# A hybrid decoder layer on one core: x instead of E at the start, more gate strips ahead of the GLU, E behind the recurrence, the last products on VectorE

## Chip, core and metric

One core of a Trainium2 chip. The metric is the device time of one execution in microseconds (us), from inputs in HBM to the output in HBM. PE is TensorE, PEld its weight loads, DVE is VectorE, ACT is ScalarE, POOL is GpSimd, SP the engine whose queue issues the DMAs.

## The reference

One layer on 1024 tokens of width 1024, batch 1, in float32 (the names are the reference's; shapes are left out):

```python
h = rms_norm(x, g_mix)
z = h @ w_in + b_in                      # 3584 columns: u_a 512, u_b 1024, gate_a 1024, gate_b 1024
y_a = s5_mixer(u_a)                      # diagonal complex SSM, then gelu and a GLU
y_b = rglru_mixer(u_b)                   # causal conv of 4, gates r and i per head, a linear recurrence
x = x + (gate_a * (y_a @ w_a_out) + gate_b * (y_b @ w_b_out)) @ w_o
h2 = rms_norm(x, g_ffn)
x = x + (silu(h2 @ w_ffn_gate) * (h2 @ w_ffn_up)) @ w_ffn_down
gate_p = sigmoid(rms_norm(x, g_ple_gate) @ w_ple_gate + b_ple_gate)
e = rms_norm(p @ w_ple, g_ple)
x = x + gate_p * e
return rms_norm(x, g_final)
```

## The kernel before

Everything is held transposed: 128 channels on the partitions, 1024 tokens along the free axis. A tile of 128 x 1024 float32 is a slot of SBUF (43 slots), and a PSUM tile of that size is one of four PSUM slots. A *strip* is 128 output channels of a product: its weights are 8 blocks of 128 x 128, loaded in two halves of 256 KB into three raw buffers.

Each factor is split in two: ScalarE makes a high part (`whi`, `xgh`, line 190 or 237), VectorE the rest (`wlo`, `xgl`, line 191 or 238). `mm3` (line 215) then does three products per block, each in two matmuls of 512 tokens, so a strip of w_in is 8 x 3 x 2 = 48 matmuls and a product of E, which has two blocks of p, is 12.

`plan` writes the work down as a list of units, in the order in which PE is to take them. `emit` (line 323) issues a unit: its weights' loads and splits a few halves ahead (`load_to`, `prep_to`), its matmuls, after the first half the evacuation of the unit before (`flush`), and after each half one `tick`, which takes every running chain (a Python generator, such as the norm's or the S5 branch's) one step further. So a chain's place among the strips is counted in ticks of 24 matmuls. Within the first `HEAD_UNITS` units, ScalarE and VectorE keep the order in which this is written; for the rest, and for PE, POOL and SP throughout, a planner fixes each engine's order before the run, by the order of issue, by when it expects the data and by `high_priority`. Each engine then works strictly in its order, and an instruction that waits holds back all behind it.

The order before is:

- **E**, p @ w_ple: eight units of 12 matmuls (lines 496 to 511). `head` (line 471) issues all loads: p, w_ple, the small tables, x. Meanwhile a chain (`x_one`, line 459) splits the eight tiles of x and sums their squares, and the S5 parameters start on POOL (`s5_params`, line 1161, instructions on 16 columns). The results go to HBM (`ed`).
- **u_a**, four strips of w_in. Their evacuation needs the norm of x (`rstd_chain`, line 370): sums on PE, the power `rs` on POOL (line 388), `dg` on VectorE, a product with ones that spreads it (line 395), and ScalarE's copy `rb` (line 400). The S5 parameters that follow are issued behind `rs`.
- **Ten gate strips** (`GATES_FIRST`), while the S5 branch runs as chains: setup of two halves (`s5_setup`, line 1319), sine tables, input products (line 1451), rotation and scans on VectorE, output products (line 1488), four steps apart (`S5_LAG`). Up to here that is 8 x 12 + 14 x 48 = 768 matmuls of `mm3`.
- The **GLU** (4 strips of 24), the first u_b strip (UB 0), and w_a_out.
- The **recurrence**: UB 1 to 7, behind UB m the gate pair `ri` of m - 2, and a gate strip behind m = 2, 3, 5, 6 (`UB_GATES`). A UB strip is evacuated by VectorE, ScalarE and VectorE again (convolution, `xc`) and split (`xch`). Each pair of channels' tiles then goes through `lru` (line 609): exponential, tanh, square root on ScalarE, products and two scans on VectorE. Behind `ri` 6 there is a gate strip, `ri` 7, and one more gate strip; then w_b_out, which needs the splits of all y_b.
- w_o, the FFN, w_down, and the gate of E at the end, whose last five strips are cut at token 768 (`TAIL_CUT`): the first part's final norm (`final_head`, line 995) runs beside the second parts' matmuls. `final_mul` (line 990) is the product of a finished tile with the final norm and its store; before, four of the first six are on POOL and two on VectorE (`FIN_FIRST`), and two more wait for `final_tail` (`FIN_LAST`).

Of the kernel before, what the change touches and what calls it, by code (L numbers as in the profile page):

```python
# [15 lines left out]
ALU = mybir.AluOpType  # L16
# [17 lines left out]
GATES_FIRST = 10  # L34
UB_GATES = (2, 3, 5, 6)
RI_LAG = 2
S5_LAG = 4
S5_STAGGER = 3
X_POOL = ()
HEAD_UNITS = 10  # L40
# [4 lines left out]
FIN_FIRST = ((0, 0), (1, 1), (2, 0), (3, 1), (4, 1), (5, 1))  # L45
FIN_LAST = (6, 7)
# [41 lines left out]
class WUnit:  # L88
# [3 lines left out]
    def __init__(self, strips, ops, out, pre=None):  # L92
        self.strips, self.ops, self.out, self.pre = strips, ops, out, pre
        self.first = None
        self.raw = self.sums = None


class Build:
# [223 lines left out]

    def emit(self, u, ahead):
        if isinstance(u, WUnit):
# [113 lines left out]
    def plan(self):  # L438
# [11 lines left out]
        pt = {}  # L450

        def p_tile(k):
            return pt[k]

        xg = {}
        xacc = []
        st = {}

        def x_one(k):
            t = st.pop(("x", k))  # L460
            xg[k] = self.split(t, "xg", scale=self.v("g_mix", k))
            self.accum(xacc, t, nc.gpsimd if k in X_POOL else nc.vector)

        def x_chain():
            for k in range(8):
                x_one(k)
                yield

        wple = {}

        def head():
            t = [self.slot(name="p") for _ in range(2)]
            nc.sync.dma_start(t[0], h["pT"][0])
            self.s5p = self.small([P, 48], name="s5p")
            self.dd = self.small([32, 16, 16], name="dd")
            for i in range(2):
                wple[i] = self.slot(name="wple")
                nc.sync.dma_start(wple[i][:, :512], h["w_ple"][2 * i])
                if i == 0:
                    nc.sync.dma_start(t[1], h["pT"][1])  # L480
                    nc.sync.dma_start(self.vec, h["vec"])
                    nc.sync.dma_start(self.s5p, h["s5p"])
                    nc.sync.dma_start(self.dd, h["s5d"])
                    nc.sync.dma_start(self.ident, h["ident"])
                    nc.sync.dma_start(self.iota, h["iota"])
                nc.sync.dma_start(wple[i][:, 512:], h["w_ple"][2 * i + 1])
                for k in range(4 * i, 4 * i + 4):
                    st["x", k] = self.slot(name="x")
                    nc.sync.dma_start(st["x", k], h["xT"][k])
            for k in range(2):  # L490
                pt[k] = self.split(t[k], "p")
                self.prep_to(1)
            self.xc = self.start(x_chain())
            self.start(self.s5_all())

        def ev_e(n):
            def ev(ps):
                t = self.slot(name="e")
                if n % 2:
                    nc.scalar.activation(out=t, in_=ps, func=AF.Copy)  # L500
                else:
                    nc.vector.tensor_copy(t, ps)
                nc.sync.dma_start(self.ed[n], t)
            return ev

        for n2 in range(4):
            e = self.elem(lambda n2=n2: wple[n2 // 2][:, 512 * (n2 % 2):512 * (n2 % 2) + 512])
            for q in range(2):
                n = 2 * n2 + q
                self.add([(e, [(2 * q + k, (lambda kk=k: p_tile(kk))) for k in range(2)])], ev_e(n),  # L510
                         pre=head if n == 0 else None)


        rstd = self.rstd = {}

        def pre_in():
            self.drain(self.xc)
            self.rc = self.start(self.rstd_chain(lambda: xacc.pop(), lambda t: rstd.update({"x": t})))
# [27 lines left out]
        for m in range(4):  # L546
            self.add(w_in(m), ev_ua(m), pre=pre_in if m == 0 else None)
# [187 lines left out]
        for m in range(8):  # L735
            add_ao(m)
        for m in range(8):
            if m:
                add_ub(m)
            if m >= RI_LAG:  # L740
                add_ri(m - RI_LAG)
            if m in UB_GATES:
                add_gate()
        for m in range(8 - RI_LAG, 8):
            if m == 7:
                add_gate()
            add_ri(m)
        while gates:
            add_gate()
        self.units[-2].pre = lambda: setattr(self, "ybg", self.start(yb_split()))  # L750
# [239 lines left out]
        def final_mul(k, eng):  # L990
            x = x1[k][:, :TAIL_CUT]
            (nc.gpsimd if eng else nc.vector).tensor_tensor(out=x, in0=x, in1=rstd["z"][:, :TAIL_CUT], op=ALU.mult)  # L992
            nc.sync.dma_start(self.out[k, :, :TAIL_CUT], x)

        def final_head():
            n = TAIL_CUT
            yield from self.rstd_chain(lambda: acc3[0], lambda t: rstd.update({"z": t}), n, lag=FIN_LAG, lag2=FIN_LAG2)
            for k, eng in FIN_FIRST:
                final_mul(k, eng)
                yield  # L1000

        def final_tail(sq):
# [12 lines left out]
            nc.vector.tensor_scalar(out=ms[:, :m], in0=ps[:, :m], scalar1=1.0 / D, scalar2=EPS, op0=ALU.mult, op1=ALU.add)  # L1015
            nc.gpsimd.tensor_tensor(out=rs[:, :m], in0=ms[:, :m], in1=self.mhalf[:, :m], op=ALU.pow)
            mark = nc.vector.tensor_tensor(
                out=dg[:, :m], in0=self.ident.unsqueeze(1).to_broadcast([P, m, P]),
                in1=rs[:, :m].unsqueeze(2).to_broadcast([P, m, P]), op=ALU.mult)
            with self.tc.issue_after(mark.ins):  # L1020
                for k in FIN_LAST:
                    final_mul(k, 0)
# [14 lines left out]
        def ev_pg(n, t0, t1):  # L1037
            w = t1 - t0

            def ev(ps):  # L1040
# [10 lines left out]
                nc.vector.tensor_tensor(out=t, in0=ps[:, :w], in1=rstd["g"][:, t0:t1], op=ALU.mult)  # L1051
# [3 lines left out]
                nc.vector.tensor_tensor(out=x, in0=x, in1=e, op=ALU.add)  # L1055
# [6 lines left out]
                if n == 7:  # L1062
                    if t0 == 0:
                        self.start(final_head())
                    else:
                        final_tail(s)
# [357 lines left out]
    def s5_data(self, hf):  # L1424
# [12 lines left out]
        yield  # L1437
# [134 lines left out]
```

## Time and profile before

| | |
|---|---|
| median of 3 runs | 1467.52 us (1467.17 to 1469.06) |
| the profiled execution | 1465.75 us |
| its span, first to last instruction | 1463.8 us |
| busy in the span: PE, DVE, ACT, POOL | 1415.7, 848.9, 565.6, 164.4 us |
| mean granted TensorE clock | 0.984 |

The time is that of an execution; the span is what the trace covers of it, and all positions below are us from its start. In rows of the timeline, the first number is the start, the second the length, then engine, line, operation, tiles and count; in brackets stands how long the engine was idle before, and whose end released it.

### The profile page before, as it was taken

To read this page: it belongs to the slowest core of one execution; us is meant where nothing else is said; L and a number is where in the kernel's file an instruction comes from. 1 tells how busy PE (TensorE), PEld (TensorE's weight loads), DVE (VectorE), ACT (ScalarE), POOL (GpSimd) and SP (SyncE) were. 2 spreads that over 40 slices of the span, in tenths; PEclk is the share of its full clock that TensorE was granted. 3 is DMA by queue.
4 is the path that set the end of the run, shared out by engine and by line. 5 is a ranking of instruction groups with operands and counts; after the bars stand their busy time and mean duration, and the time that the engine had idled before them with its cause. 6 is when DMAs were issued, how large, how long until landed. Compare 5 with 4: busy or idle time off the path is not lost.

```text
span 1463.8 us, 16823 instructions
## 1 busy us (share of the span) xinstructions
PE 1415.7 (97%) x6586; PEld 1171.3 (80%) x6586; DVE 848.9 (58%) x988; ACT 565.6 (39%) x722; POOL 164.4 (11%) x250
## 2 busy tenths in 40 slices
PE   8999989999988899998999999999999999999995
PEld 6788877888877688886888888888888888888885
DVE  7367873635766864466655555556666234266586
ACT  7233236313566831353433333333335341133343
POOL 7910700000000000000000000000000021012243
PEclk9999989999999999999999999999999999999997
DMA  8324334441221653352122222222217342233122
GB/s 323 108 101 118 105 85 144 162 169 58 86 78 67 222 180 129 128 175 86 55 75 78 81 87 86 87 87 87 87 65 274 135 158 66 74 101 106 60 94 115
DMA packets 72046, 167.68 MB, mean 115 GB/s; under 512 B 11712, under 2 KB 23392, under 8 KB 71968
## 3 DMA queue, kind: packets, MB, share of 16 engines
q1 hardware_dynamic: 71968, 166.62, 33.7%
q8 instruction: 51, 0.84, 0.2%
q14 instruction: 27, 0.22, 0.0%
HBM read 121.37 MB, written 44.04 MB: 113 GB/s over the span
## 4 chain that ended last, share of the span: by engine, by line
PE 78%; issue 5%; DVE 5%; ACT 5%; POOL 4%; SPq 1%; DMA 1%; DVEq 0%; POOLq 0%; ACTq 0%
PE mm L223 46%; PE mm L315 28%; PE sm L1488 1%; PE sm L1493 1%; PE sm L223 1%; POOL x L992 1%; SPq L1392 1%; ACT ri L603 1%; POOL el L1054 0%; DVE yb L634 0%; DVE x L1055 0%; PE sm L380 0%; DVE xc L583 0%; SPq L1432 0%; DVE el L1045 0%
## 5 line engine op out<-in xcount | busy, mean ns | idle before, releaser
L190 ACT ACTIVATE whi<-raw 128x512 fp32r<-128x512 f32 (+1 forms) x158 | 97.2, 617 | 358.1 <-PE mm L223 298.4
L315 PE MATMUL mm<-twh,whi 128*128 128x512 f32 x528 | 206.4, 391 | 1.3 <-ACT pc L293 1.0
L315 PE MATMUL mm<-twl,whi 128*128 128x512 f32 x528 | 205.9, 390 | 0.8 <-DVE twl L235 0.8
L315 PE MATMUL mm<-twh,wlo 128*128 128x512 f32 x528 | 202.4, 390 | 0.0
L191 DVE TENSOR_TENSOR wlo<-raw,whi 128x512 fp32r<-128x512 f32 (+1 forms) x158 | 111.8, 710 | 130.1 <-ACT whi L190 130.1
L223 PE MATMUL mm<-xgh,whi 128*128 128x512 f32 x448 | 140.3, 394 | 4.4 <-ACT ri L603 4.4
L223 PE MATMUL mm<-xgh,wlo 128*128 128x512 f32 x448 | 138.7, 391 | 0.9 <-DVE wlo L191 0.9
L223 PE MATMUL mm<-xgl,whi 128*128 128x512 f32 x448 | 139.2, 392 | 0.0
L315 PEld LDWEIGHTS mm<-twh,whi 128*128 128x128 f32 x528 | 99.4, 188 | 23.1 <-ACT pc L293 1.4
L315 PEld LDWEIGHTS mm<-twl,whi 128*128 128x128 f32 x528 | 99.4, 188 | 21.8 <-DVE twl L235 1.1
L315 PEld LDWEIGHTS mm<-twh,wlo 128*128 128x128 f32 x528 | 99.4, 188 | 20.8
L415 POOL TENSOR_TENSOR acc<-acc,sq 128x1024 f32<-128x1024 f32 (+1 forms) x18 | 43.2, 2400 | 613.5 <-DMA raw<-w_down 468.6
L177 ACT ACTIVATE whi<-wr 128x512 fp32r<-128x512 f32 x110 | 69.4, 631 | 107.5 <-PE mm L315 104.0
L223 PE MATMUL mm<-vh,wlo 128*128 128x512 f32 x352 | 108.9, 390 | 0.0
L223 PE MATMUL mm<-vl,whi 128*128 128x512 f32 x352 | 108.4, 389 | 0.0
L223 PE MATMUL mm<-vh,whi 128*128 128x512 f32 x352 | 108.4, 389 | 0.0
L223 PEld LDWEIGHTS mm<-xgh,whi 128*128 128x128 f32 x448 | 84.4, 190 | 23.1 <-ACT ri L603 4.9
L223 PEld LDWEIGHTS mm<-xgh,wlo 128*128 128x128 f32 x448 | 84.5, 189 | 19.0 <-DVE wlo L191 1.3
L223 PEld LDWEIGHTS mm<-xgl,whi 128*128 128x128 f32 x448 | 84.7, 189 | 17.9 <-issue 0.2
L178 DVE TENSOR_TENSOR wlo<-wr,whi 128x512 fp32r<-128x512 f32 x110 | 74.4, 684 | 27.5 <-ACT whi L177 27.4
L223 PEld LDWEIGHTS mm<-vh,whi 128*128 128x128 f32 x352 | 66.1, 188 | 13.9 <-issue 0.2
L223 PEld LDWEIGHTS mm<-vh,wlo 128*128 128x128 f32 x352 | 66.1, 188 | 13.9 <-issue 0.2
(389 smaller groups left out, 2451.7 us busy)
## 6 DMA issues: line engine op xcount, KB each, us to landing
raw<-w_in SPq DMA_DIRECT2D x56, 256.0 KB, 2.7
wr<-w_gate SPq DMA_DIRECT2D x22, 512.0 KB, 4.9
wr<-w_up SPq DMA_DIRECT2D x22, 512.0 KB, 3.5
vd<-fv SPq DMA_DIRECT2D x22, 512.0 KB, 3.0
vr<-vd SPq DMA_DIRECT2D x22, 512.0 KB, 5.6
raw<-w_down SPq DMA_DIRECT2D x32, 256.0 KB, 2.7
el<-ed SPq DMA_DIRECT2D x16, 512.0 KB, 4.4
x<-xT SPq DMA_DIRECT2D x8, 512.0 KB, 7.6
```

Of the source, the lines that this page charges most:

```text
L177: nc.scalar.activation(out=hi, in_=src, func=AF.Copy)
L178: nc.vector.tensor_tensor(out=lo, in0=src, in1=hi.bitcast(F32), op=ALU.subtract)
L190: nc.scalar.activation(out=hi[:, :w], in_=raw[:, :w], func=AF.Copy)
L191: nc.vector.tensor_tensor(out=lo[:, :w], in0=raw[:, :w], in1=hi[:, :w].bitcast(F32), op=ALU.subtract)
L223: nc.tensor.matmul(ps[:, t - t0:e - t0], w, v[:, t:e], start=(first and q == 0), stop=(last and q == 2),)
L315: nc.tensor.matmul(bank[b], w[:, k * P:(k + 1) * P], v, start=start and k == 0 and p == 0, stop=k == 3 and p == 2, skip_group_check=True)
L415: eng.tensor_tensor(out=a, in0=a, in1=s, op=ALU.add)
L603: nc.scalar.activation(out=t, in_=ps[q], func=AF.Sigmoid, bias=self.v(b, m))
L992: (nc.gpsimd if eng else nc.vector).tensor_tensor(out=x, in0=x, in1=rstd["z"][:, :TAIL_CUT], op=ALU.mult)
L1392: nc.sync.dma_start(km[i][16 * j:16 * j + 16, :, (7 - j) * 16:P], ks[16 * i:16 * i + 16, :, 0:(j + 1) * 16])
L1488: nc.tensor.matmul(ps[:, o:o + P], km[hh][:, pr, :], us[q][:, 2 * i + hh, :], start=True, stop=False)
L1493: nc.tensor.matmul(ps[:, o + 1:o + P], G(w[hs, pr]), x[hs, pr * P:pr * P + 127], start=False, stop=last)
```

## The change

The program begins with a new unit, `HeadUnit`: the two first strips of w_in at once, tile by tile of x (`emit_head`). SP issues the small vector, the first weight half and x 0 first. The squares' sums stand two tiles behind the splits. The norm's chain starts with the last tile. ScalarE and VectorE keep their written order for two units (the head and the third strip) instead of ten.

E's eight products move: two behind UB 4 and `ri` 2, six behind `ri` 7, as the last work ahead of w_b_out; p and w_ple are loaded from UB 4 on. Twelve gate strips instead of ten stand ahead of the GLU; the one behind UB 2 and the last one are gone from the recurrence, so 16 x 48 = 768 matmuls lie ahead of the GLU. The S5 input products come one step later behind their tables (`PSV_LAG`). All `final_mul` go to VectorE: two when the norm is there, six placed behind named instructions of the last two strips and of `final_tail`.

```diff
-GATES_FIRST = 10
-UB_GATES = (2, 3, 5, 6)
+GATES_FIRST = 12
+UB_GATES = (3, 5, 6)
+UB_E = (4,)
+PSV_LAG = 2
-HEAD_UNITS = 10
+HEAD_UNITS = 2
+HEAD_STRIPS = 2
-FIN_FIRST = ((0, 0), (1, 1), (2, 0), (3, 1), (4, 1), (5, 1))
-FIN_LAST = (6, 7)
+FIN_FIRST = (0, 1)
...
+    def emit_head(self, u):
+        n = len(u.elems)
+        u.pre()
+        ps = [self.ps_mm() for _ in range(n)]
+        for k in range(8):
+            u.load(k)
+            for i in range(n):
+                e, w = u.elems[i][k // 4], slice(k % 4 * P, k % 4 * P + P)
+                self.mm3(ps[i], self.hi[e][:, w], self.lo[e][:, w], u.use(k), k == 0, k == 7)
+            self.tick()
+        self.pend = lambda: [ev(p) for ev, p in zip(u.evs, ps)]
...
         def head():
...
+            nc.sync.dma_start(self.vec, h["vec"])
+            self.load_to(1)
+            load_x0(0)
+            self.load_to(2)
...
+            nc.sync.dma_start(self.s5p, h["s5p"])
+            for k in (1, 2):
+                load_x0(k)
...
+            self.start(self.s5_all())
+
+        def head_tile(k):
+
+            if k == 0:
                 self.prep_to(1)
...
+            t = st["x", k]
+            xg[k] = self.split(t, "xg", scale=self.v("g_mix", k))
+            if k == 0:
+                self.prep_to(HEAD_STRIPS)
+                self.load_to(2 * HEAD_STRIPS)
+                for i in range(5, 8):
+                    load_x0(i)
+            if k == 2:
+                self.prep_to(2 * HEAD_STRIPS)
+                self.load_to(2 * HEAD_STRIPS + 3)
+            if k >= 5:
+                self.prep_to(2 * HEAD_STRIPS + k - 4)
+            if k >= 2:
+                acc_x(k - 2)
+            if k == 7:
+                acc_x(6)
+                acc_x(7)
+                self.rc = self.start(self.rstd_chain(lambda: xacc.pop(), lambda t: rstd.update({"x": t})))
...
+        def p_chain():
+            t = [self.slot(name="p") for _ in range(2)]
+            for k in range(2):
+                nc.sync.dma_start(t[k], h["pT"][k])
+            yield
+            yield
+            for k in range(2):
+                pt[k] = self.split(t[k], "p")
+                yield
...
         for m in range(8):
             if m:
                 add_ub(m)
+                if m == UB_E[0]:
+                    self.units[-1].pre = lambda: setattr(self, "pgen", self.start(p_chain()))
             if m >= RI_LAG:
                 add_ri(m - RI_LAG)
             if m in UB_GATES:
                 add_gate()
+            if m in UB_E:
+                for _ in range(2):
+                    add_e(ne)
+                    ne += 1
...
+        for n in range(ne, 8):
+            add_e(n)
...
+        def final_after(k, ins):
+            while "z" not in rstd:
+                self.step(self.fin)
+            with self.tc.issue_after(ins.ins):
+                final_mul(k)
...
-                nc.vector.tensor_tensor(out=t, in0=ps[:, :w], in1=rstd["g"][:, t0:t1], op=ALU.mult)
+                i = nc.vector.tensor_tensor(out=t, in0=ps[:, :w], in1=rstd["g"][:, t0:t1], op=ALU.mult)
+                if t0 and n >= 6:
+                    final_after(2 * n - 10, i)
...
-                nc.vector.tensor_tensor(out=x, in0=x, in1=e, op=ALU.add)
+                i = nc.vector.tensor_tensor(out=x, in0=x, in1=e, op=ALU.add)
+                if t0 and n >= 6:
+                    final_after(2 * n - 9, i)
...
         yield from tb
-        yield
+        for _ in range(PSV_LAG):
+            yield
```

In `final_tail`, tile 6 stands behind the mean's product (line 1015) and tile 7 behind `dg` (line 1017).

## Rows read from the trace of the kernel before

**Rows 1.** The page: the span, and part 1, each engine's busy time
```profile
span 1463.8 us, 16823 instructions
...
PE 1415.7 (97%) x6586; PEld 1171.3 (80%) x6586; DVE 848.9 (58%) x988; ACT 565.6 (39%) x722; POOL 164.4 (11%) x250
```

**Rows 2.** Table of stretches, whole core: length, busy time by engine, clock, DMA share
```profile
180.00:250.00 70.00, 64.70 (x375) 53.51 (x374) 38.09 (x39) 29.62 (x27) 1.61 (x2) 0.93 0.39 112
395.00:412.00 17.00, 13.08 (x51) 10.28 (x51) 13.51 (x14) 8.21 (x9) 0.00 (x0) 0.90 0.21 76
455.00:512.00 57.00, 48.13 (x196) 38.30 (x196) 41.59 (x36) 45.10 (x46) 0.00 (x0) 0.94 0.46 163
...
700.00:1100.00 400.00, 400.00 (x1767) 331.12 (x1766) 235.80 (x359) 145.82 (x236) 0.00 (x0) 1.00 0.24 81
```

**Rows 3.** List of PE's waits: what it waited for, us in total, times, longest
```profile
PE mm L223 <- ACT ri L603: 4.4, 1, 4.4
...
PE sm L1488 <- DVE q L1462: 3.7, 1, 3.7
```

**Rows 4.** Timeline of the head and S5's begin, by engine; POOL's table of stretches
```profile
6.08 2.08 PE L223 MATMUL mm<-ph,whi 128*128 128x512 f32 x4 [6.08 <-ACT whi L190]
...
15.40 1.22 DVE L502 COPY e<-mm 128x1024 f32<-128x1024 f32 x1 [3.29 <-PE mm L223]
...
16.54 1.28 DVE L238 SCALAR_TENSOR_TENSOR xgl<-x,vec,xgh 128x1024 fp32r<-128x1024 f32 x1
...
16.80 1.13 POOL L1104 TENSOR_SCALAR ep<-ep 128x16 f32<-128x16 f32 x1
...
20.70 1.23 DVE L415 TENSOR_TENSOR acc<-acc,sq 128x1024 f32<-128x1024 f32 x1
...
7.00:44.70 37.70, 33.37 (x79) 1.00 0.77 295
39.70:44.70 5.00, 4.31 (x21) 1.00 0.33 105
...
44.72 1.67 POOL L388 TENSOR_TENSOR rs<-ms,mhalf 128x8 f32<-128x8 f32 x1
...
46.42 1.23 DVE L389 TENSOR_TENSOR dg<-ident,rs 128x1024 f32<-128x1024 f32 x1 [5.82 <-POOL rs L388]
...
47.79 1.96 PE L395 MATMUL sm<-dg,ones 128*128 128x512 f32 x4 [2.73 <-DVE dg L389]
49.19 1.03 PE L223 MATMUL mm<-xgh,whi 128*128 128x512 f32 x2
...
71.80 0.83 POOL L1316 COPY bd<-bb 64x256 f32<-64x256 f32 x2
...
84.22 1.22 DVE L1338 TENSOR_TENSOR qr<-ar,bb 128x1024 f32<-128x1024 f32 x1
```

**Rows 5.** Timeline of DVE, S5: the second half's input products are read
```profile
191.39 0.69 DVE L1459 TENSOR_TENSOR q<-sm,pw 128x512 f32<-128x512 f32 x1 [3.99 <-ACT pw L1421]
```

**Rows 6.** Timeline of ACT behind UB 7: the split ahead of the gates' evacuation
```profile
464.12 1.06 ACT L234 ACTIVATE xch<-xc 128x1024 fp32r<-128x1024 f32 x1 [4.79 <-DVE xc L583]
```

**Rows 7.** Timeline of DVE and POOL in the tail
```profile
1440.73 0.42 DVE L1054 TENSOR_TENSOR el<-el,pg 128x256 f32<-128x256 f32 x1 [0.57 <-ACT pg L1052]
...
1442.81 3.48 DVE L992 TENSOR_TENSOR x<-x,rb 128x768 f32<-128x768 f32 x2 [0.28 <-ACT rb L400]
1442.85 8.99 POOL L992 TENSOR_TENSOR x<-x,rb 128x768 f32<-128x768 f32 x4 [6.01 <-ACT rb L400]
...
1447.19 1.05 DVE L1054 TENSOR_TENSOR el<-el,pg 128x256 f32<-128x256 f32 x1 [0.57 <-ACT pg L1052]
1448.27 1.91 DVE L1055 TENSOR_TENSOR x<-x,el 128x256 f32<-128x256 f32 x1
...
1450.66 1.46 DVE L415 TENSOR_TENSOR acc<-acc,sq 128x256 f32<-128x256 f32 x1 [0.15 <-ACT sq L413]
...
1455.78 1.82 DVE L992 TENSOR_TENSOR x<-x,rb 128x768 f32<-128x768 f32 x2
```

More of the change, by code (lines that the diff above doesn't have):

```diff
@@ L95, in __init__ @@
         self.raw = self.sums = None
+class HeadUnit:
+    def __init__(self, elems, pre, load, use, evs):
+        self.elems, self.pre, self.load, self.use, self.evs = elems, pre, load, use, evs
 class Build:
@@ L457, in plan, with load_x0, acc_x @@
         st = {}
[L459 to L466, printed above, removed]
-                yield
-        wple = {}
+        rstd = self.rstd = {}
+        def load_x0(k):
+            st["x", k] = self.slot(name="x")
+            nc.sync.dma_start(st["x", k], h["xT"][k])
+        def acc_x(k):
+            self.accum(xacc, st.pop(("x", k)))
@@ L490, in head @@
-            for k in range(2):
-                pt[k] = self.split(t[k], "p")
-                self.prep_to(1)
[L493 to L518, printed above, removed]
+            nc.sync.dma_start(self.s5p, h["s5p"])
@@ L544, in ev_ua, with w_ple, ev_e, ev @@
             return ev
-        for m in range(4):
-            self.add(w_in(m), ev_ua(m), pre=pre_in if m == 0 else None)
+        n = HEAD_STRIPS
+        first = [[None] * 2 for _ in range(n)]
+        for q in range(2):
+            for m in range(n):
+                first[m][q] = self.elem(h["w_in"][m][:, 512 * q:512 * q + 512])
+        self.units.append(HeadUnit(first, head, head_tile, lambda k: xg[k], [ev_ua(m) for m in range(n)]))
+        for m in range(n, 4):
+            self.add(w_in(m), ev_ua(m))
+        pt, wple, e_elem = {}, {}, {}
+        def w_ple(n2):
+            if n2 // 2 not in wple:
+                t = wple[n2 // 2] = self.slot(name="wple")
+                for i in range(2):
+                    nc.sync.dma_start(t[:, 512 * i:512 * i + 512], h["w_ple"][n2 // 2 * 2 + i])
+            return wple[n2 // 2][:, 512 * (n2 % 2):512 * (n2 % 2) + 512]
+        def p_chain():
[7 more added lines that the diff above has]
+                yield
+        def ev_e(n):
+            def ev(ps):
+                t = self.slot(name="e")
+                if n % 2:
+                    nc.scalar.activation(out=t, in_=ps, func=AF.Copy)
+                else:
+                    nc.vector.tensor_copy(t, ps)
+                nc.sync.dma_start(self.ed[n], t)
+            return ev
+        def pre_e():
+            self.drain(self.pgen)
+        def add_e(n):
+            if n % 2 == 0:
+                e_elem[n // 2] = self.elem(lambda: w_ple(n // 2))
+            q = n % 2
+            self.add([(e_elem[n // 2], [(2 * q + k, (lambda kk=k: pt[kk])) for k in range(2)])], ev_e(n),
+                     pre=pre_e if n == 0 else None)
         def ev_ga(m):
@@ L736, in plan @@
             add_ao(m)
+        ne = 0
         for m in range(8):
@@ L1014, in final_tail @@
             dg = self.slot(shape=(P, 8, P), name="dg")
[L1015 removed]
+            i = nc.vector.tensor_scalar(
+                out=ms[:, :m], in0=ps[:, :m], scalar1=1.0 / D, scalar2=EPS, op0=ALU.mult, op1=ALU.add)
             nc.gpsimd.tensor_tensor(out=rs[:, :m], in0=ms[:, :m], in1=self.mhalf[:, :m], op=ALU.pow)
[L1017 removed]
+            final_after(6, i)
+            i = nc.vector.tensor_tensor(
                 out=dg[:, :m], in0=self.ident.unsqueeze(1).to_broadcast([P, m, P]),
                 in1=rs[:, :m].unsqueeze(2).to_broadcast([P, m, P]), op=ALU.mult)
[L1020 to L1022 removed]
+            final_after(7, i)
             rp = self.ps_sm()[:, :n]
```

41 lines of the change are left out of this document (13 added, 28 removed).

## Prediction

> **What bounds the kernel now.** I read the page's engine line first: the span is 1463.8 us and PE is busy for 1415.7 us of it [rows 1]. The change neither adds nor removes a matmul of the strips or of E, so what it can win is time in which PE stands or runs slowly: 1463.8 - 1415.7 = 48.1 us of standing, and what the clock costs. For the latter I read the table of stretches [rows 2]: where the granted clock is 1.00 (700 to 1100 us, PE busy for all 400) it costs nothing; a mean of 0.93 over 70 us is 10 us at the lower level (1.2 GHz), worth 70 x 0.07 = 4.9 us; 17 x 0.10 = 1.7 us around 400; 57 x 0.06 = 3.4 us around 480. In these rows the clock falls behind a stop of PE. The same 400 us give the unit price: 1767 matmuls, 0.226 us each, so a strip's 48 cost 10.9 us and an E product's 12 cost 2.7 us.
>
> The same page shows PEld at 1171.3 us, 80% [rows 1]. The Trainium skill (Trainium Kernel Development and Optimization, Performance Expectations) says to judge distance to the roofline by utilization and weight-load busy share, not by matmul busy time; by that rule some 290 us of the array would be open to a better order. The stretch at 1.00 speaks against using it here: with PE never waiting, PEld is at 331 of 400 us too, so a reorder has only the stops to win.
>
> PE's busy time in these stretches gives the stops: 70.0 - 64.7 = 5.3 us in the S5 stage, of which the list of PE's waits names 3.7 before the output products (the other 1.6 is ahead of the GLU); 17.0 - 13.1 = 3.9 at 403; 57.0 - 48.1 = 8.9 from 455 on, 4.4 of them on the recurrence's gates, 4.5 where w_b_out begins [rows 2, 3].
>
> **The head.** Now PE starts at 6.1 on E, whose 8 x 12 = 96 matmuls fill the time in which VectorE and ScalarE split x; one strip follows, and PE is through 144 matmuls at 49.2, behind the broadcast [rows 4]. In the change PE starts with x itself. Tile 0 leaves on SP third instead of first, at about 1.6 us, and needs one more weight split on VectorE; I put the first matmul at 7, +1 us, hidden as follows. Up to the last square VectorE has 8 splits of 1.28, 7 weight splits (half as wide, 0.69 for such a pass), 7 additions of 1.23 [rows 4, 5]: 23.7 us, from 7 to about 30.5. PE needs 96 x 0.226 = 21.7 us and, trailing by a tile, is through two strips at about 29. The eight x transfers now have no p, w_ple or E stores ahead of them and wait for nothing. Then PE has one more strip (to 40, as four PSUM slots are then two strips, this one and the norm's), and must have the broadcast: `rs` on POOL, `dg`, its matmuls. PE's order is fixed ahead, so the broadcast's matmuls stand somewhere inside that strip; I take its middle.
>
> When is `rs`? POOL has 79 instructions ahead of it now, from 7 to 44.7, the last 21 in 5.0 us once VectorE is quiet (0.24 each), while one takes 1.13 us that starts beside a split on VectorE and ends with it [rows 4]. In the new head VectorE is full of those from 7 to 30.5: 22 instructions let about 22 pass, its gaps some 5 more, so 27 are done. If `rs` stays last, 52 x 0.24 = 12.5 us follow and `dg` begins at 30.5 + 12.5 + 1.7 = 44.7. If the planner, which has `rs` at high priority and the sum ready at 32, puts it ahead of what is left, `dg` begins at 37 to 40. The trace favours the latter: VectorE's first S5 setup ran at 84.2 although POOL's last input for it was there at 72.6 [rows 4], so the order seems to count POOL as slower than it ran. I take 39: + 1.2 (`dg`) + 0.1 + 1.4 (matmuls) + 12 x 2 x 0.226 = 5.4 (rest of the strip) + 1.7 (a clock drop, as behind the stop at 403) = 48.8, against 49.2. **Head: 0**, bounds -4 (no drop, matmuls at the strip's end) and +7.
>
> **S5.** Between broadcast and GLU there are as many matmuls as before (144 done, 768 before the GLU in both), so twelve gate strips instead of ten cost nothing and only make up for E. What differs: the S5 chain steps 48 matmuls earlier, and PSV_LAG puts its input products one step (24 matmuls, 5.4 us) later behind their tables. Now the products of the second half hold two PSUM slots until VectorE reads them, from 191.4 on, when the sine table comes (it had waited 4.0 for that); the first half's output products need those slots, and PE stops 3.7 us and then runs at 1.2 GHz for some 10 [rows 2, 3, 5]. 5.4 later is more than 3.7, so this stop and its 4.9, with the 1.6 at the GLU, could go: -10. But VectorE is what feeds this stage, and a chain that is pulled forward meets it elsewhere; bounds -10 and +3. I take **-4**, the stop of 3.7 itself and little of the clock, since the wait for the sine table is not removed and the short matmuls there may run at 1.2 GHz as they do now.
>
> **Recurrence.** After UB 7 nothing changes: PE waits there for ScalarE's evacuation of two gate pairs, behind `xch` [rows 6]; 4.4 plus its drop stays. At 403 two E products will stand ahead of the strip before that stop: 5.4 us of cover against 3.9 + 1.7, but VectorE, on whose queue that stop hangs, gets 2 x 1.23 (splits of p), 0.69 and 1.22 (evacuation) more [rows 4], 4.4 us, and each product takes a PSUM slot. I take 0, bounds -5 and +6. At the end six E products (16.3 us) replace one gate strip (10.9 us) between the last recurrence gates and w_b_out. Now that stretch loses 4.5 and half of 3.4 for the clock, 6.2 in all [rows 2], while ScalarE works through tanh, square root and the splits of yb. 5.4 us more cover, against three evacuations (1.06 for a pass of that size [rows 6]) and one weight split more on ScalarE, less a sigmoid, about 2.6 us: **-3**, bounds -6 and 0. The stores of E and later loads are as many as before. Loading p and w_ple late puts four 512 KB-equivalents on SP's queue in a stretch where DMA is at 21 to 46% [rows 2]: nothing.
>
> **Tail.** Now POOL multiplies four tiles (8.99 us) beside VectorE's last products. Against their unhindered times, VectorE's pair takes 3.48 for 1.82, then 1.05 for 0.42, 1.91 for 0.42, 1.46 for 0.42: 4.8 us, all on the way to the last norm [rows 7]. Four more products on VectorE cost 4 x 0.91 = 3.6, of which I count 2.1 as fitting into its waits for ScalarE's sigmoids, PE's sums and POOL's power (the first of them is 0.57). **-3**, bounds -4.5 and 0. The last stores leave as before.
>
> Sum: 0 - 4 + 0 - 3 - 3 = -10; as every order here is the planner's, I count half a microsecond against it: -9.5. The profiled execution took 1465.75 us (span 1463.8, 1.95 around it), 1.8 below the median of the three runs, 1467.52. So 1456.3 by its own time, **1458.0** as a median. A measurement of this kernel tells 0.2%, 2.9 us, from no change.
>
> **Rivals.**
> (a) *The two E products in the recurrence cost VectorE's queue more than they cover*, 0.15. Their 4.4 us there come ahead of the evacuation that PE waits for at 403, and the longer stop costs another 1.7 of clock: +6.1 on the forecast, 1464.1. For it: VectorE is busy for 13.5 of the 17 us around that stop [rows 2]. Against it: the splits of p need nothing of the recurrence and can fill gaps before it.
> (b) *The orders change nothing in the middle*, 0.10: S5's and the end's stops come back at another instruction since VectorE and ScalarE bind there; only the tail's 3 remain, 1464.5.
> (c) *The broadcast comes late*, 0.15, slower. Place: POOL, 7 to 45 us. If `dg` begins at 46.4 as now [rows 4], PE, with its PSUM slots full, is through 144 matmuls at 46.4 + 1.2 + 0.1 + 1.4 + 5.4 + 1.7 = 56.2, 7.1 later, and S5, whose parameters wait behind the same queue, wins nothing: +7 - 3 = +4, 1471.5. It decides from a `dg` at 42.4, where the head's loss equals the tail's gain. For it: POOL's 1.13 us in place of 0.24 [rows 4]. The Trainium skill (SBUF — State Buffer, Who interferes with whom) has a lock of one port pair, by which a VectorE instruction with two SBUF inputs shuts out a GpSimd instruction that reads SBUF until it ends; by that rule, the trace agrees (0.24 us alone, 1.13 beside a split), the new head holds POOL longest where `rs` needs it. Against it: `rs` may overtake.
>
> **How the numbers follow.** Forecast 0.60, with its own range 1449 to 1463; (a) 0.15, (b) 0.10, (c) 0.15. The range reaches from -21 (head -4, S5 -10, end -4, tail -3) to +3.5: 1446 to 1471, which leaves out the worse half of (c) and the best orders. Faster by over 0.2%: 0.58 of the forecast, 0.06 of (a), 0.05 of (b), 0.69. Within: 0.02, 0.07 and 0.05 of the same, 0.14. Slower: 0.15 of (c), 0.02 of (a), 0.17.
>
> **What would show it.** Head: PE at 144 strip matmuls near 49, `rs` with parameter instructions of POOL still behind it; (c) if it is the last and a stop of over 6 us stands around 40. S5: no stop ahead of the first output products, clock 1.00 around 200. End: w_b_out begins with less than 3 us of stops. Tail: 0.42 us instructions on VectorE, POOL free until its `rs`, and some 3 us less from VectorE's first final product to the span's end (1442.8 to 1463.8 now). The forecast is wrong if stops of PE add up to over 45 us again.

## The result and the profile after

The changed kernel takes **1481.72 us** (median of 4 runs, 1479.98 to 1482.43) where the kernel before took 1467.35 beside it: a ratio of 1.009, 95% interval 1.0073 to 1.0108, slower by 14.4 us. Forecast was 1458.0, with a range up to 1471. The profiled execution took 1481.28 us, its span is 1479.2.

The page of the changed kernel, span and PE's busy time, against [rows 1]:

```profile
span 1479.2 us, 16813 instructions
...
PE 1417.9 (96%) x6586; PEld 1172.5 (79%) x6586; DVE 846.3 (57%) x992; ACT 564.7 (38%) x721; POOL 139.7 (9%) x246
```

The instructions of PE are as many as before. It stands for 1479.2 - 1417.9 = 61.3 us where it stood for 48.1: 13.2 of the 15.4 us that the span grew. The prediction had named stops of over 45 us as its sign of being wrong. The rest is slower running. Where it happens, I read from positions of PE's instructions in the two timelines. A stretch's own work differs only where the last column says so (0.226 us a matmul):

| stretch, from first to last of PE | before | after | change | of it moved work |
|---|---|---|---|---|
| start to the 145th strip or E matmul | 49.2 | 57.5 | +8.3 | none |
| from there to the GLU's first (240.78, now 246.00) | 191.6 | 188.6 | -3.0 | none |
| GLU, UB 0, w_a_out, UB 1, to the first `ri` (338.83, now 346.69) | 98.1 | 100.7 | +2.6 | none |
| recurrence, to the end of the last `ri` (481.46, now 495.07) | 142.6 | 148.4 | +5.8 | two E products in, a gate strip out: -5.4 |
| end, to the first of w_o (585.92, now 605.40) | 104.5 | 110.3 | +5.9 | six E products in, a gate strip out: +5.4 |
| w_o, FFN, gate of E, to the last strip's end (1446.73, now 1464.64) | 860.8 | 859.2 | -1.6 | none |
| tail, to the span's end | 17.1 | 14.6 | -2.5 | none |

So the head lost 8.3, the recurrence 5.8 + 5.4 = 11.2 (it lost 5.8 with 5.4 us less of work), the end won nothing, S5 gave back at and behind the GLU what it won, and the tail won 2.5. The list of PE's waits (us in total, times, longest) names the new stops, against [rows 3]:

```profile
PE mm L232 <- ACT ph L243: 14.2, 1, 14.2
...
PE mm L232 <- ACT zh L243: 6.3, 1, 6.3
...
PE mm L232 <- ACT e L585: 4.6, 1, 4.6
PE mm L232 <- ACT ri L655: 4.4, 1, 4.4
PE sm L418 <- DVE dg L412: 4.4, 2, 3.9
```

The S5 stop of [rows 3] (3.7, behind `q`) is gone; the stop on `ri` behind UB 7 is the same 4.4. The table of stretches (length, busy time of PE, PEld, DVE, ACT, POOL, then granted clock and DMA) of the kernel before in two stretches not shown above, then of the changed kernel, to be held against [rows 2] too:

```profile
0.00:60.00 60.00, 50.13 (x210) 39.98 (x211) 34.57 (x39) 32.27 (x37) 47.72 (x137) 1.00 0.64 237
380.00:412.00 32.00, 28.08 (x118) 22.71 (x117) 23.84 (x22) 17.84 (x20) 0.00 (x0) 0.95 0.26 91
```

```profile
0.00:60.00 60.00, 46.18 (x176) 35.97 (x177) 30.37 (x35) 30.02 (x32) 47.50 (x139) 0.91 0.43 158
180.00:250.00 70.00, 63.70 (x381) 52.89 (x380) 38.04 (x41) 28.77 (x28) 0.00 (x0) 0.96 0.42 125
380.00:412.00 32.00, 17.80 (x72) 14.28 (x71) 21.37 (x18) 15.55 (x16) 0.00 (x0) 0.79 0.20 74
```

Around 400 us the changed kernel stands 14.2 us in one piece where the kernel before stood 3.9. The clock's 0.79 looks like 32 x 0.21 = 6.7 us more, but most of it costs nothing. The same table of the changed kernel, cut at the stop's ends and at the clock's steps, shows why:

```profile
387.65:391.61 3.96, 0.00 (x0) 0.00 (x0) 3.96 (x4) 0.00 (x0) 0.00 (x0) 1.00 0.59 202
391.61:401.85 10.24, 0.00 (x1) 0.00 (x1) 7.79 (x7) 3.20 (x4) 0.00 (x0) 0.50 0.19 74
401.85:405.26 3.41, 3.41 (x8) 2.73 (x9) 2.53 (x3) 3.38 (x4) 0.00 (x0) 0.50 0.00 0
```

The clock fell inside the stop, and of its 13.65 us at 1.2 GHz (0.50) PE runs only in the last 3.41. That costs half of 3.41, 1.7 us, and behind the stop of 3.9 the kernel before paid the same 1.7. What the changed kernel loses at this place is the 10.3 us of longer standing.

The head has 34 matmuls less in its first 60 us, and its clock is 0.91 where it was 1.00: PE runs for 9.3 us of the head at 1.2 GHz, which costs 4.7 of the 8.3.

**The head.** Timeline of the changed kernel, all engines, in order of start; to be read against [rows 4]:

```profile
7.78 1.65 PE L232 MATMUL mm<-xgh,whi 128*128 128x512 f32 x3 [7.78 <-ACT xgh L246]
...
17.11 1.17 POOL L1169 TENSOR_TENSOR ep<-ep,er 128x16 f32<-128x16 f32 x1
...
33.03 1.21 DVE L438 TENSOR_TENSOR acc<-acc,sq 128x1024 f32<-128x1024 f32 x1
34.30 0.94 PE L403 MATMUL sm<-ones,acc 128*128 128x1 f32 x7 [2.15 <-DVE acc L438]
36.28 0.17 DVE L410 TENSOR_SCALAR ms<-sm 128x8 f32<-128x8 f32 x1 [2.04 <-PE sm L403]
...
44.52 0.22 POOL L1178 TENSOR_TENSOR ep<-ep,em 128x16 f32<-128x16 f32 x1
44.70 1.67 POOL L411 TENSOR_TENSOR rs<-ms,mhalf 128x8 f32<-128x8 f32 x1
46.40 1.23 DVE L412 TENSOR_TENSOR dg<-ident,rs 128x1024 f32<-128x1024 f32 x1 [9.95 <-POOL rs L411]
47.77 3.75 PE L418 MATMUL sm<-dg,ones 128*128 128x512 f32 x4 [3.89 <-DVE dg L412]
```

In the kernel before, `ms` came here:

```profile
40.44 0.17 DVE L387 TENSOR_SCALAR ms<-sm 128x8 f32<-128x8 f32 x1 [0.90 <-PE sm L380]
```

So `ms` is ready at 36.5 us instead of 40.6, but `rs` comes at 44.70, directly behind the last of the 79 parameter instructions, at the place and time that it had before (44.72). Beside a split on VectorE such an instruction still takes 1.17 us on POOL, where it takes 0.22 at 44.52. The sum that came 4 us earlier waits on POOL.

**The recurrence.** Timelines of VectorE, ScalarE and PE of the changed kernel around the stop of 14.2 us:

```profile
386.45 2.29 DVE L686 TENSOR_TENSOR_SCAN yb<-a,ri 128x1024 f32<-128x1024 f32 x1
...
390.37 2.29 DVE L686 TENSOR_TENSOR_SCAN yb<-a,ri 128x1024 f32<-128x1024 f32 x1
392.57 1.20 DVE L533 TENSOR_TENSOR u<-mm,rb 128x1024 f32<-128x1024 f32 x1
...
393.81 1.15 ACT L630 ACTIVATE u<-u,vec 128x1024 f32<-128x1024 f32 x1 [7.14 <-DVE u L533]
399.79 1.06 ACT L243 ACTIVATE xch<-xc 128x1024 fp32r<-128x1024 f32 x1 [4.84 <-DVE xc L635]
400.76 1.99 ACT L243 ACTIVATE ph<-p 128x1024 fp32r<-128x1024 f32 x2
...
401.85 2.08 PE L232 MATMUL mm<-ph,whi 128*128 128x512 f32 x4 [14.20 <-ACT ph L243]
```

p's loads were issued at 364.75. Its split `ph`, which E's matmuls need, stands in ScalarE's order behind `u` and `xch` of UB 4. ScalarE waits 7.14 us for VectorE's `u`, and VectorE reads `u` out of PSUM only after the pair's gating products and both scans (`yb`).

### The profile page after: what moved, and what is told of

It is laid out like the page before. It is cut to its first block, busy times and chain, and to the rows that moved or that the text cites. A ratio compares the mean times of both kernels' runs of the same rounds, so it can differ in the third digit from the quotient of the medians.

```text
span 1479.2 us, 16813 instructions
## 1 busy us (share of the span) xinstructions
PE 1417.9 (96%) x6586; PEld 1172.5 (79%) x6586; DVE 846.3 (57%) x992; ACT 564.7 (38%) x721; POOL 139.7 (9%) x246
## 4 chain that ended last, share of the span: by engine, by line
PE 83%; ACT 5%; issue 4%; DVE 4%; POOL 3%; DMA 1%; SPq 0%; DVEq 0%; ACTq 0%; POOLq 0%
PE mm L232 50%; PE mm L324 28%; PE sm L232 1%; PE sm L1564 1%; PE sm L1522 1%; PE sm L1559 1%; DVE xc L635 1%; DVE x L1123 1%; PE sm L418 1%; ACT ri L655 0%; ACT a L672 0%; DVE el L1111 0%; ACT sq L436 0%; PE sm L403 0%; ACT ri L669 0%
```

## The experiments

Two questions: is the recurrence's loss the place of `ph` in ScalarE's order, or the E products themselves; and is the head's loss the place of `rs`? With them go the change's other parts, one at a time on the kernel before. Each ratio is to the kernel before, run beside it (1467.5 to 1468.5 us), with its 95% interval.

**p split earlier** (`e1_p_early`).

```diff
-                if m == UB_E[0]:
+                if m == UB_E[0] - 1:
```

> The changed kernel with p's load and split started one up-projection unit earlier, so that ScalarE's order has the two halves ph ahead of u(4). Theory A (the 14.20 us stop at 387.65 is a place in ScalarE's order: ph lies behind u(4) and xch(4), which wait for VectorE, while p had landed 18 us before): the two E products then run in that stop, it shrinks to at most the 3.9 us that the kernel before had at 402.91, and its 13.65 us at 1.2 GHz shrink to some 3.4: 10 us of stop and 5 of clock, 1481.3 - 15 = 1466, between 1462 and 1470. Rival B (the two E products load VectorE and ScalarE with their split and their copies, and whatever place they have, the next ri waits as much later): the stop moves behind the E products with its length, 1478 to 1482.

1484.39 us, 1.0101 (1.0085 to 1.0117): no gain, as rival B has it, though not at B's place. `ph` came 32 us earlier (368.6 us), and the stop came back in two pieces. Timelines of PE and VectorE of this run:

```profile
394.67 1.19 PE L232 MATMUL mm<-ph,whi 128*128 128x512 f32 x2 [5.42 <-DVE u L533]
...
406.99 1.22 PE L232 MATMUL mm<-xgh,whi 128*128 128x512 f32 x2 [6.87 <-ACT ri L655]
...
393.32 1.20 DVE L533 TENSOR_TENSOR u<-mm,rb 128x1024 f32<-128x1024 f32 x1
```

My theory fell. The first E product runs at 386.4; the second needs nothing more of p, weights or ScalarE, yet waits for VectorE's reading of `u`, and the strip after it for ScalarE's of `ri`. What is short is the accumulator: of the four PSUM slots, UB 4, the two halves of `ri` 2 and the first E product hold one each, and the second E product starts 0.15 us after `u` has been read (393.32 + 1.20).

**All E products at the end** (`e2_e_behind`).

```diff
-UB_E = (4,)
+UB_E = ()
...
-                if m == UB_E[0]:
+                if m == 6:
```

> The changed kernel with no E product inside the recurrence: all eight behind the last gate strip. Theory A: the stop at 387.65 goes back to the 3.9 us and 3.4 us of low clock that the kernel before had there, the later stops keep their sizes; the two E products (5.2 us of TensorE at full clock) move to the end, where their copies wait on ScalarE as the six do now (4.56 us): 1481.3 - 15 = 1466, and not slower than the run with the earlier split by more than 3. Rival B (the recurrence needs the E products as cover, so that stops of their 5.2 us turn up at ri 4 to 7 in their place): 1471 to 1475.

1471.78 us, 1.0022 (1.0013 to 1.0031): 9.9 less than the changed kernel. PE's waits show the stop back at its old size, and the one behind UB 7 a little longer than 4.4:

```profile
PE mm L232 <- ACT ri L655: 5.3, 1, 5.3
PE mm L232 <- ACT e L585: 4.6, 1, 4.6
PE sm L232 <- ACT ri L655: 3.9, 1, 3.9
```

The recurrence misses the two E products for 0.8 us, at the stop behind UB 7; with them it lost ten. At the end eight wait for their own copies exactly as six did. The stops are theory A's, the time lies in B's range: A's 1466, like that of the run before, counted 5 us of clock for the long stop, of which the rows above show 1.7, no more than the short stop has.

**The tail alone** (`e3_tail_only`), the kernel before with the diff's part from `final_mul` on.

> The kernel before with only the tail of the change: the last products all on VectorE, each behind a named instruction. From the last strip's end to the span's end the two kernels' traces show 17.09 and 14.60 us. Theory A (the tail is a term of its own): 2.5 us less, 1464.9 against 1467.4. Rival B (the tail's 2.5 us come from another clock or state of the queues that the earlier stages leave, such as the stop at 1446.73 that is 5.46 us in the one and 2.35 in the other): less than 1 us, 1466.4 to 1467.4.

1465.82 us, 0.9983 (0.9974 to 0.9993): 2.5 less, as the traces' 17.1 against 14.6 say. The tail is a term of its own.

**The S5 delay alone** (`e4_psv_only`).

```diff
-        yield
+        for _ in range(2):
+            yield
```

> The kernel before with only the one unit more of delay ahead of the S5 products of each half. Theory A (the stop of 3.70 us at 190.32 and the 10.24 us at 1.2 GHz behind it, worth 5.1, go; the S5 chain ends no later): 1467.4 - 8.8 = 1458.6. Rival B (the S5 chain is what the GLU waits for: its stop, 1.59 us at 239.19, grows by what the other gives back, as the changed kernel's 6.30 us at 239.70 suggests, and drops the clock there): 1464 to 1467.4. Rival C (the second half's products come later by a whole strip of 15.6 us and the GLU waits for most of it): slower, 1470 to 1480.

1467.92 us, 0.9997 (0.9988 to 1.0006): nothing, rival B. The stop at 190 is gone from its trace; the GLU's wait is this (first row), and the next rows are the stretch around the GLU's start, in the kernel before (second fence) and here (third):

```profile
PE mm L223 <- ACT zh L234: 6.3, 1, 6.3
```

```profile
225.00:250.00 25.00, 23.41 (x128) 19.23 (x127) 7.13 (x7) 16.11 (x13) 0.00 (x0) 1.00 0.49 144
```

```profile
225.00:250.00 25.00, 18.70 (x96) 14.99 (x94) 6.17 (x6) 15.54 (x12) 0.00 (x0) 0.80 0.47 132
```

23.41 - 18.70 = 4.7 us of standing came in where 3.7 went out. Of the 10.2 us at 1.2 GHz here, PE stood for 4.1, so the clock costs 3.1; at the old stop PE ran for 8.9 of 10.2, which cost 4.4. So 7.8 came in where 8.1 went out. Timeline of ScalarE ahead of the GLU, first before, then in the changed kernel:

```profile
233.33 0.63 ACT L190 ACTIVATE whi<-raw 128x512 fp32r<-128x512 f32 x1 [3.16 <-PE mm L223]
...
235.27 4.09 ACT L668 ACTIVATE z<-y 128x1024 f32<-128x1024 f32 x2
```

```profile
239.29 0.63 ACT L199 ACTIVATE whi<-raw 128x512 fp32r<-128x512 f32 x1 [4.81 <-PE mm L232]
239.94 1.28 ACT L720 ACT_TABLE_LOAD   x1
241.23 3.87 ACT L720 ACTIVATE z<-y 128x1024 f32<-128x1024 f32 x2
244.90 2.00 ACT L243 ACTIVATE zh<-z 128x1024 fp32r<-128x1024 f32 x2
```

One step later in S5, the Gelu `z` falls behind the last weight split, which waits 4.81 us for PE. From there table load, two Gelu passes and the split of `z` are in sequence, and PE has run out of strips at 239.7. Its y had been asked for at 219.5 and a y load took 5.3 us, so by the trace it is a place in ScalarE's order once more. No run moves the Gelu ahead of that split, so this cause is read from the trace and not shown.

**rs earlier** (`e5_rs_early`), from the run with all E products at the end: the 24 instructions of the sine and cosine go behind `rs`.

```diff
-        k, t2, r, re, w = T("k"), T("t2"), T("r"), T("re"), T("w")
...
-        yield
         while "x" not in self.rstd:
             yield
+        with self.tc.issue_after(self.rs):
+            k, t2, r, re, w = T("k"), T("t2"), T("r"), T("re"), T("w")
...
```

> The run with all E products at the end (1471.8), with GpSimd's sine and cosine rows of the S5 parameters (24 instructions) put behind rs, so that rs follows 55 of the 79 parameter rows instead of all. Theory A (the head's loss of 7 to 8 us is rs standing last in GpSimd's order): rs ends near 38 instead of 46.4, dg near 40, the stop on dg (2.20 us) and the clock drop behind it go, the 145th strip matmul starts near 53 instead of 56.6, and as the GLU's start has followed that matmul in all runs so far (188.5 us behind it), the end comes 3 to 6 us earlier: 1466 to 1469. Rival B (the S5 chain starts from those GpSimd rows and sets the GLU's start): the 145th matmul comes earlier by as much, the stop at the GLU grows by as much, 1471 to 1473.

1467.70 us, 0.9995 (0.9984 to 1.0006): 4.1 less in the median than the run that it was put into. Its head, POOL, VectorE and PE:

```profile
40.23 1.67 POOL L411 TENSOR_TENSOR rs<-ms,mhalf 128x8 f32<-128x8 f32 x1
...
41.93 1.23 DVE L412 TENSOR_TENSOR dg<-ident,rs 128x1024 f32<-128x1024 f32 x1 [6.00 <-POOL rs L411]
...
43.30 1.96 PE L418 MATMUL sm<-dg,ones 128*128 128x512 f32 x4
```

`dg` begins 4.5 us earlier than in the changed kernel, PE does not wait for it at all, and the 145th matmul starts at 50.1 instead of 56.6. The stop at the GLU stays at 6.30, so S5 came forward with it: theory A. Not all of these 6.5 us are the edit's. Ahead of `rs`, PE stood 2.28 for the sum here and 3.07 there, and then ran 3.4 us at 1.2 GHz here and 6.8 there, which is 2.5 together. The other 4.0 are the stop of 2.20 on `dg` and the 1.7 of clock behind it, and agree with the median.

**Four E products ahead of the GLU** (`e6_e_glu`), four at the end; p's loads start three strips ahead of them.

```diff
+E_FIRST = 4
...
         for m in range(GATES_FIRST):
+            if m == GATES_FIRST - 1:
+                for n in range(E_FIRST):
+                    add_e(n)
             add_gate()
...
```

> The run with all E products at the end, with four of the eight put ahead of the last gate strip before the GLU, 10.4 us of TensorE work where it stops for 6.30 us on S5. Theory A (the GLU waits for S5 whose chain is not TensorE's, and the end's stop is E's own copies on ScalarE behind the recurrence's last step, so that four products are cover enough there): the GLU's stop of 6.30 and its 6.83 us at 1.2 GHz go, the end keeps one stop of 4 to 5 us: 1471.8 - 9 = 1463, between 1461 and 1466. Rival B (the copies of E stand in ScalarE's and VectorE's order between the S5 rows and delay them by their own 1 us each, or the end, with 10.4 us less of cover, waits for the recurrence): 1469 to 1476.

1467.03 us, 0.9993 (0.9974 to 1.0011): 4.7 less than with all at the end. (The two spans, 1470.7 and 1462.0, differ by 8.7, but they belong to the second slowest of ten executions there and to the fastest of ten here.) The median lies between the two theories. The GLU's stop is 2.87 instead of 6.30 and the clock is 1.00 from 225 to 255, but the end has three stops of 3.5 us together at w_b_out.

**Both** (`e7_rs_e_glu`).

> Both edits together. If theory A holds for both and they add: 1457 to 1462. If the S5 chain sets the GLU's start (rival B of the first), the second edit's four products cover that too: 1460 to 1464. If the end lacks the cover: 1468 to 1474.

1462.79 us, 0.9958 (0.9941 to 0.9975): 5.7 faster than the kernel before, 9.0 below the run with all E at the end; the edits add (4.1 + 4.7).

**The rest of the change on the old head** (`e8_gate_lag_tail`): E where it was, the S5 delay and the tail as in the runs above, 11 gate strips ahead of the GLU.

```diff
-GATES_FIRST = 10
-UB_GATES = (2, 3, 5, 6)
+GATES_FIRST = 11
+UB_GATES = (3, 5, 6)
...
```

> The kernel before, its head and its E products where they were, with the rest of the change: the one unit of delay in S5, the tail, and one gate strip more ahead of the GLU (11; the one taken from the recurrence is that behind up-projection 2). Theory A (the delay's 6.30 us stop at the GLU, with 10.24 us at 1.2 GHz, needs a strip of 15.6 us as cover; the recurrence loses only 0.8 us by that gate, 5.26 against 4.44, as the run with E at the end shows): 1467.4 - 6.3 - 5.1 + 0.8 + 1.7 - 2.5 = 1456, between 1453 and 1460; then what the change lost lies in its head and in the E products alone. Rival B (S5 runs on TensorE's strips and the GLU waits whatever stands ahead, or the gate strip is missed in the recurrence by more): 1463 to 1468.

1464.63 us, 0.9970 (0.9959 to 0.9982). The gain beyond the tail's 2.5 is 1.4, and theory A fell: with a strip more ahead of it the GLU's stop is 6.30 as without. The S5 chain steps with the strips, so it and the Gelu's place moved along. Taking the gate behind UB 2 out cost the recurrence no stop (3.92 and 4.43).

**u ahead of the scans** (`f1_p_early_u`), from the run with p split earlier. A test of the accumulator: VectorE's gating products and scans go behind the next `u`, so that its PSUM slot comes free earlier.

```diff
-                u = scaled(ps, "x", "u")
+                u = self.slot(name="u")
+                self.u_ins = nc.vector.tensor_tensor(out=u, in0=ps, in1=need_rstd("x"), op=ALU.mult)
...
             yield
+            for _ in range(2 if m0 < 6 else 0):
+                yield
             for m in ms:
-                nc.vector.tensor_tensor(out=ri[m, 1], in0=ri[m, 1], in1=th.pop(m), op=ALU.mult)
+                with self.tc.issue_after(self.u_ins.ins):
+                    nc.vector.tensor_tensor(out=ri[m, 1], in0=ri[m, 1], in1=th.pop(m), op=ALU.mult)
```

> The changed kernel with p split early (1484.4), and in VectorE's order of each recurrence pair the two gating products and the two scans put behind the next up-projection's u instead of ahead of it. Theory A (TensorE has four accumulators of 128x1024; at 388.6 us u(4), the two of ri(2) and the first E product hold them, the second E product waits 5.42 us until VectorE has read u(4), and the next strip 6.87 us until ScalarE has read ri, because u(4) stands behind two products and two scans in VectorE's order): u(4) is read at some 384 instead of 393.3, the stop of 5.42 goes, that of 6.87 falls to 0 to 3, their 13.65 us at 1.2 GHz to at most 3.4: 1484.4 - 14 = 1470, between 1467 and 1474. Rival B (VectorE and ScalarE have too much work there in any order, the E products' copies and split among it): the stops move to the scans' readers, the later ri or the w_b_out products: 1479 to 1485.

1471.90 us, 1.0036 (1.0023 to 1.0050): 12.5 less than without in the medians, 9.5 by the two ratios; theory A by its time. VectorE, PE and ScalarE of this run, then ScalarE of the next run, `f2_best_u`, which has the same order and no E product in the recurrence:

```profile
385.89 1.22 DVE L630 TENSOR_TENSOR u<-mm,rb 128x1024 f32<-128x1024 f32 x1
...
387.95 0.62 PE L232 MATMUL mm<-ph,whi 128*128 128x512 f32 x2
...
398.87 1.22 PE L232 MATMUL mm<-xgh,whi 128*128 128x512 f32 x2 [5.32 <-ACT ri L656]
...
397.70 2.12 ACT L656 ACTIVATE ri<-sm,vec 128x1024 f32<-128x1024 f32 x2
```

```profile
399.42 2.12 ACT L662 ACTIVATE ri<-sm,vec 128x1024 f32<-128x1024 f32 x2
```

`u` is read at 385.9, before the second E product asks for its accumulator, and the stop of 5.42 does not occur; no instruction was removed. The other, for `ri`, went only from 6.87 to 5.32 where I expected 3 at most.

What is left of it is the accumulator too. Here PE has ended `ri` 2 at 388.1 and ScalarE reads it at 397.70, 9.6 us later; in `f2_best_u` these are 390.1 and 399.42, 9.4 us. So E's own work hardly delays that read. But in `f2_best_u` PE has a strip of 10.9 us to run in the free slot meanwhile and does not stop, and here two E products of 2.7 fill two slots and leave it standing. With `u` late the read comes 15.0 us behind `ri` 2 in the kernel before and in `e2_e_behind`, 16.4 in the changed kernel and 19.3 in `e1_p_early`, so there E's work delays it by 1.4 to 4.3 us as well.

Part of the gain has nothing to do with E: the next run and the last show this order worth 5 to 7 us without E products there. By the length of the recurrence less E's own 5.4 us, the two E products cost 143.0 - 133.9 = 9 us with `u` late (the changed kernel and `e2_e_behind`) and 133.4 - 127.3 = 6 with `u` early (this run and `f2_best_u`). No run changes the number of slots.

**The same in the kernel with both edits** (`f2_best_u`).

> The same order of u in the run with rs early, four E products ahead of the GLU and four at the end (1462.8). Theory A: the stops of 3.92 us at 400 and 4.43 us at 460 in its recurrence, both for an ri that stands behind u and its xc, fall to 0 to 1 each, with the low clock behind them: 1462.8 - 10 = 1453, between 1450 and 1457. Rival B (the scans, later by 6 to 8 us, hold up the last pair and so w_b_out): 1460 to 1466.

1455.97 us, 0.9918 (0.9898 to 0.9938): 6.8 less than without, theory A. The stop of 3.92 at 400 is gone. The one behind UB 7 is still 4.44, against the expectation.

**rs earlier on the old head** (`f3_oldhead`), the edit of `e5_rs_early` in `e8_gate_lag_tail`.

> The run with the old head, the S5 delay, one gate strip more ahead of the GLU and the tail (1464.6), with rs put ahead of GpSimd's sine and cosine rows as in the run with rs early. Theory A (rs last in GpSimd's order costs either head): its stop on dg, 2.92 us at 45.84, goes, with up to 1.7 of clock: 1460 to 1462.5. Rival B (the old head's first strip waits for the sum of squares, not for rs): 1464 to 1465.

1460.49 us, 0.9949 (0.9934 to 0.9964): 4.1 less than without it, theory A. `rs` last on POOL cost the kernel before as well: the stop on `dg`, 2.73 in [rows 4], is gone and the 145th matmul starts at 46.3.

**u ahead of the scans on the old head** (`g1_oldhead_u`).

> The old head with rs early, E's products where the kernel before has them, the S5 delay, one gate strip more ahead of the GLU and the tail (1460.5), with u ahead of the gating products and the scans in VectorE's order. Theory A (the order of u is worth the same with any head, the stop of 3.92 us at 399.71 goes and those at 458 and 492 keep their sizes): 1460.5 - 7 = 1454, between 1451 and 1457, so the move of E's products to the back is needed for none of the gain. Rival B (the E products at the end and ahead of the GLU are what makes room in the other run, where the same edit took 6.8 us): 1458 to 1461.

**1455.13 us, 0.9914 (0.9884 to 0.9943)**, the lowest median of the study, 13.3 below the kernel before and 5.4 below `f3_oldhead`, theory A; `f2_best_u` is the same within the intervals. The stop of 3.92 is gone, the one behind UB 7 keeps its 4.43. E's products stand here where the kernel before has them. Of the change it keeps the tail, the S5 delay and one gate strip ahead of the GLU.

## Why the prediction was wrong

*Head: predicted 0 (bounds -4 and +7), measured +8.3.* The step that failed is "I take 39" for `dg`. The argument was that the planner counts POOL as slow and so lets `rs` overtake; it put `rs` last, and `dg` began at 46.40, in [rows 4] at 46.42. This is rival (c) in place and price: it gave 46.4 for `dg` and 56.2 for the end of 144 matmuls, against 57.5 here. Its stop of over 6 us came in two pieces, 2.15 at the sum and 3.89 at `dg`. That the place of `rs` is a cause is shown by `e5_rs_early`, which reorders POOL alone and ends the wait for `dg`; in the changed kernel that wait is 3.89 and the clock behind it 3.0. It is not the whole of the 8.3, since the kernel before had `rs` in the same place and stood 2.73 for it. With `rs` early on both, the 145th matmul starts at 50.1 behind the new head and at 46.3 behind the old one, so 3.8 are the new head's own: PE starts 1.2 later (7.15 against 5.92), waits 2.28 for the sum and then runs for 3.4 us at 1.2 GHz. The prediction had no stop for the sum: it took VectorE's last square to be in at 30.5, and it came at 34.2.

*S5: predicted -4 (bounds -10 and +3), measured -3.0 ahead of the GLU and +2.6 behind it, -0.4 in all.* The stop went as said. The step that failed is that nothing was put against it at the GLU, whose 1.6 was to stay or to go: it grew to 6.30. `e4_psv_only` shows this part by itself at nothing. That two more gate strips cost nothing was right, and that they cover nothing at the GLU (6.30 with 10, 11 or 12 of them) was not seen.

*Recurrence: predicted 0 (bounds -5 and +6), measured +11.2.* The step that failed is "5.4 us of cover against 3.9 + 1.7". I wrote that each product takes a PSUM slot and gave that no price. An E product keeps PE busy for 2.7 us and holds its slot, as any strip does, until VectorE or ScalarE has come to it in its order; a strip keeps PE busy for 10.9 in the same slot. PE then stood 14.2 instead of 3.9 at 400 us; the other 0.9 is clock, behind UB 7. Rival (a) had the sign, and VectorE's queue as the place, at 6.1; the cause it gave, the 4.4 us of added work on that queue, is not the main one: `f1_p_early_u` keeps that work, reads `ri` 2 as soon as `f2_best_u` without it, and still stops 5.32 for want of a slot. The place of `ph`, which the trace suggests first, was one layer above it: with `ph` early the accumulators stopped PE for 12.3 us.

The Trainium skill (Perfetto Trace Analysis, Optimization Strategy) says that a gap that keeps coming back on the engine that should be saturated can mean too little PSUM for the next tile. The trace of `e1_p_early` agrees in the cause (5.42 us on `u`, 6.87 on `ri`, both reads of PSUM), though these are two different stops and not one that repeats.

*End: predicted -3 (bounds -6 and 0), measured +0.4.* The stops at w_b_out did go. In their place PE waits for the copies of E itself, 4.6 us on ScalarE's: the copy stands there among the last pair's exponentials, tanh and square roots. The step that failed is that I had counted the copies as ScalarE's load (2.6 us) and not as something that PE waits for. This is read from the trace; no run here moves the copies alone.

*Tail: predicted -3 (bounds -4.5 and 0), measured -2.5*, by the table and by `e3_tail_only`. VectorE's second-part instructions of 256 columns take 0.42 us throughout, as the prediction asked, where [rows 7] have 1.05 to 1.91.

The sum of the terms was -10 and came out as 8.3 - 0.4 + 11.2 + 0.4 - 2.5 = +17.0, less 1.6 between w_o and the last strip, where the same stop behind w_o is followed by a shorter stretch at 1.2 GHz. The range was too short at the top by more than a term: (a) and (c) stood as alternatives, though one lies at 40 us and the other at 400 and nothing keeps both from coming. Together, with S5 and the end at nothing, they give 7 + 6 - 3 = +10, 1477.5, still 4 below what was measured. The prediction's prices of the clock (4.9, 1.7 and 3.4) count low clock during which PE stood; by PE's running at 1.2 GHz they are 4.4, 1.7 and 2.9. And (c)'s 56.2 is 7.0 behind 49.2, not 7.1. Neither changes the outcome.

## What to carry to other kernels

Work put into a stop as cover needs an accumulator for as long as its readers take, so count cover by accumulator: a short product is poor cover where few tiles rotate and its readers' queues are full. Before moving work towards a stop, follow in each in-order queue what stands ahead of the instruction that frees the resource; here moving a read ahead of scans that PE did not wait for was worth 5 to 10 us in three kernels, and moving one small power ahead of parameters 4 in two. Price a clock drop by how long PE runs at the lower level, and not by the mean of a stretch in which it also stands. Rivals that sit in different stages add; the range has to hold their sum.

## What the runs showed of the hardware that was not expected

The clock's price of a stop is not fixed by the stop. The S5 stop is 3.7 us in [rows 3] and 3.71 in the run with the tail alone, whose part of the table of stretches is this:

```profile
180.00:250.00 70.00, 64.70 (x353) 53.40 (x352) 35.46 (x37) 27.04 (x26) 2.36 (x3) 0.85 0.40 113
```

The clock is 0.85 where [rows 2] have 0.93, with the same work in this stage and the same stop. PE runs for 19.4 us at 1.2 GHz here and for 8.9 there, a difference of 5.3 us in time. That is twice the 2.5 us that this run was to show; its gain stands in the median of 11 runs, and not in that profile, whose span of 1465.0 is above the 1463.8 of before.

Nor is the price fixed by the stop's length. The changed kernel's stop of 14.20 us and the stop of 3.9 at the same place in the kernel before both cost 1.7 us of clock, since behind each PE ran for 3.4 us at 1.2 GHz.
